# Batches of two, four and four chunks, all prepared ahead of v: a change of order in a hybrid DeltaNet and retention layer

## The chip, the cores and the metric

The kernel runs on one core of one Trainium2 chip. A core has a matrix engine (PE, with its weight loads shown apart as PEld), a vector engine (DVE), a scalar engine (ACT), a general engine (POOL) and a queue engine (SP) that mostly issues DMAs. The metric is the device time in microseconds of one execution; the time of a kernel is the median of its runs.

## The reference

One layer of a diffusion backbone: 256 context tokens and 1024 latent tokens of width 1024, all in fp32. What matters here is group A of the mixer, the gated delta rule with four heads of width 128, run in both directions:

```
qkv_a = short_conv(qkv_a, conv_w)          # 5 taps, then silu; context and latents apart
q, k, v = split(qkv_a)                     # (T, 4, 128) each
q = l2_normalize(q) * HEAD_DIM ** -0.5;  k = l2_normalize(k)
A   = strict_lower(kb @ k.T * decay)       # per chunk and head, kb = beta * k
u, w = solve(I + A, [v * beta, kb * exp(G)])
v_new = u - w @ S                          # a scan over the chunks
o     = q_dec @ S + (q @ k.T * decay) @ v_new
S     = g_last * S + k_dec.T @ v_new
```

Group B is a retention over the same tokens, with rotary angles on its q and k (`rq`, `rk`). Both groups get a norm and a gate (`z` for group A, `rg` for B), then follow an output projection, a residual, a SwiGLU feed-forward and a last norm.

## The kernel before

The kernel uses chunks of 128 tokens: chunks 0 and 1 are the context, 2 to 9 the latents. The forward scan takes 0, 1, 2 ... 9, the backward scan 1, 0, 9 ... 2. The inverse of I + A is computed for every chunk, head and direction, in batches of chunks, in four kinds of steps:

- `pre(t)`, line 719, prepares a chunk: it loads k (`kc`) and, for latents, q (`qc`), multiplies k with k (`kk`, line 724) and q with k (`kq`, line 729) on PE; for each direction it loads a broadcast row of decays (`gw`, 732), masks it on POOL (736), takes its exponential on ACT (740), multiplies on DVE (`ut`, 744, and `sp`, 746) and stores `ut` into the DRAM tensor `un` of its batch and `sp` into the packed scan input `sd`.
- `invert(b)`, line 757, loads the diagonal 32x32 blocks of the batch, one block per partition (`yr`, 765), copies them into `L` (772 on ACT, 773 on DVE) and solves them all at once on DVE: 31 steps of a multiplication (779) and a subtraction (781) whose row length depends on the step and not on the number of chunks. A copy `XT` (783) and four stores into `xd` end it.
- `merge(b)`, line 806, loads `un` into `U` (797) and the block inverses into `U` and `t64` (801, 802; each row piece of these two and of `yr` is 32 numbers long), and builds the whole inverse from the blocks by small matmuls (821 to 848) with evacuations on DVE and ACT. It ends with a store into `sd`.
- `solve(b)`, line 855, is `pre` for each chunk of the batch, then `invert`.

Between them stand the four convolution blocks of v (`conv_block(8 + h, ...)`, 866): projection matmuls from `hhi`, `hlo` with split weights (606 to 608), two copies on ACT (609, 610), four more taps on DVE (616), Silu on ACT (619), transpositions on PE (870), copies (872) and stores. Then come the token-major projections: the gate `z` (groups 8 and 9), the first two scan steps, `rk` (2 and 3) and `rq` (4 and 5). They share the PSUM tag `pa` (three banks) with v's transpositions; preparation and merges take tag `pb` (three), the convolution `pc` (two).

Order. The text gives each instruction its place; a planner at build time (`schedule_with_timeline_sim=True`, line 1665) orders every engine's instructions by a simulated timeline, so work from further down can be filled in where an engine would stand still. On the chip each engine then takes its instructions in that fixed order. Buffers come from pools that are opened and closed in the text; a new pool can lie where a closed one lay, and its tiles then wait for those that were there.

In the text before, the order is `solve(0)`, `solve(1)`, the four blocks of v, `pre` of batch 2, `merge(0)`, `invert(2)`, `merge(1)`, `merge(2)`, then `z`. The batches are [0, 1, 2, 9], [3, 8, 4, 7] and [5, 6]. The pool `GP` holds the preparation's buffers, `GI` those of the inverses. The merges' pool `GM` lies on the right side, where v's pool `CV` was; a further pool `G2` on the left holds `U` and `t64` of batch 1, so that two merges have buffers at once.

Of the kernel before, what the change touches and what calls it, by code (L numbers as in the profile page):

```python
# [8 lines left out]
F32 = mybir.dt.float32  # L9
# [8 lines left out]
P = 128  # L18
# [7 lines left out]
H = 4  # L26
# [12 lines left out]
def build(nc, tc, ap, dbg=None, stop=None, marks=None):  # L39
# [3 lines left out]
    def pool(name, bufs=1, side=None, space=None):  # L43
        kw = {}
        if side is not None:
            kw["side"] = side
        if space is not None:
            kw["space"] = space
        if space is not DRAM:
            kw["reuse_waits"] = "tile"  # L50
        es = ExitStack()
        p = es.enter_context(tc.tile_pool(name=name, bufs=bufs, **kw))
        root.push(es)
        p_close[id(p)] = es
        return p
# [3 lines left out]
    def close(p):  # L59
        p_close.pop(id(p)).close()  # L60
# [5 lines left out]
    def checkpoint(name):  # L66
        if dbg is not None:
            marks.append((name, int(nc.cur_bb.bb.instructions[-1].name.split("-")[-1])))
        if stop == name:
            raise Stop()  # L70
# [120 lines left out]
    try:  # L191
# [519 lines left out]
        GI = pool("gi")  # L711
        GP = pool("gp")

        BATCH = [[0,1,2,9],[3,8,4,7],[5,6]]
        where = {t: (b, c) for b, ch in enumerate(BATCH) for c, t in enumerate(ch)}

        un = [dr.tile([P, 2, len(ch) * H, P], F32, tag="un%d" % b, name="un%d" % b) for b, ch in enumerate(BATCH)]

        def pre(t):
            b, c = where[t]  # L720
            kc = load(GP, kd[t], "kc", 2)
            pk = bank_b("kk")
            for h in range(H):
                T.matmul(pk[:, h * P:(h + 1) * P], kc[:, h, :], kc[:, h, :], start=True, stop=True)
            if t >= 2:
                qc = load(GP, qd[t - 2], "qc", 2)
                pq = bank_b("kq")
                for h in range(H):
                    T.matmul(pq[:, h * P:(h + 1) * P], kc[:, h, :], qc[:, h, :], start=True, stop=True)
            for d in range(2):  # L730
                gw = GP.tile([P, H, P], F32, tag="gw", name="gw", bufs=2)
                SY.dma_start(gw.rearrange("p h i -> p (h i)"),
                             grow_d[c8(t, d), :].rearrange("a b -> (a b)").partition_broadcast(P))
                e = GP.tile([P, H, P], F32, tag="e", name="e", bufs=2)
                sg = 1 if d == 0 else -1
                G.affine_select(out=e, in_=gw, compare_op=ALU.is_ge, fill=FAR, base=0,
                                pattern=[[0, H], [sg, P]], channel_multiplier=-sg)
                for h in range(H):
                    col = t * 8 + d * 4 + h
                    S.activation(e[:, h, :], e[:, h, :], AF.Exp, bias=sm["nG"][:, col:col + 1])  # L740
                if t >= 2:
                    sp = GP.tile([P, 2, H, P], F32, tag="sp", name="sp", bufs=2)
                ut = GU.tile([P, H, P], F32, tag="ut", name="ut", bufs=2)
                V.tensor_tensor(ut.rearrange("p h i -> p (h i)"), pk, e.rearrange("p h i -> p (h i)"), ALU.mult)
                if t >= 2:
                    V.tensor_tensor(sp[:, 0].rearrange("p h i -> p (h i)"), pq, e.rearrange("p h i -> p (h i)"), ALU.mult)
                SY.dma_start(un[b][:, 1 - d, c * H:(c + 1) * H, :], ut)
                if t >= 2:
                    S.activation(gw, gw, AF.Exp)
                    G.tensor_tensor(sp[:, 1], gw, qc, ALU.mult)  # L750
                    SY.dma_start(sd[t, :, 8 - 8 * d:10 - 8 * d], sp.rearrange("p a h i -> p a (h i)"))
# [5 lines left out]
        def invert(b):  # L757

            nc_ = len(BATCH[b])
            nu = nc_ * H  # L760
            nb = 4 * nu
            xd = xds[b] = dr.tile([4 * nb, 1024], F32, tag="xd%d" % b, name="xd%d" % b)
            yr = GI.tile([P, 1024], F32, tag="yr", name="yr", bufs=1)
            for k in range(4):
                SY.dma_start(yr[k:2 * nb:4].rearrange("r (i j) -> r i j", j=32),
                             un[b][q32[k]].rearrange("i e u j -> (e u) i j")[:, :, q32[k]])
            L = GI.tile([P, 1024], F32, tag="L", name="L", bufs=3)
            X = GI.tile([P, 1024], F32, tag="X", name="X", bufs=2)
            G.memset(X, 0.0)
            G.memset(X[:, 0::33], 1.0)  # L770
            m = lambda t: t[:2 * nb].rearrange("p (i j) -> p i j", j=32)
            S.activation(L[:nb], yr[:nb], AF.Copy)
            V.tensor_copy(m(L)[nb:], yr[nb:2 * nb].rearrange("p (i j) -> p j i", j=32))
            for j in range(31):
                n = 31 - j
                tmp = GI.tile([P, 256], F32, tag="tmp%d" % b, name="tmp", bufs=2)
                t3 = tmp[:2 * nb, :n * (j + 1)].rearrange("p (i c) -> p i c", c=j + 1)
                sh = [2 * nb, n, j + 1]
                V.tensor_tensor(t3, bc(m(L)[:, j + 1:, j], sh, 2), bc(m(X)[:, j, :j + 1], sh, 1), ALU.mult)
                xs = m(X)[:, j + 1:, :j + 1]  # L780
                V.tensor_tensor(xs, xs, t3, ALU.subtract)
            XT = GI.tile([P, 1024], F32, tag="L", name="XT", bufs=3)
            V.tensor_copy(m(XT), X[:2 * nb].rearrange("p (i j) -> p j i", j=32))
            for i, x in enumerate((X[:nb], XT[nb:2 * nb], X[nb:2 * nb], XT[:nb])):
                SY.dma_start(xd[i * nb:(i + 1) * nb], x)

        def blocks(b):

            nu = len(BATCH[b]) * H
            nb = 4 * nu  # L790

            def blk(dram, k):
                return dram.rearrange("(u b) (i j) -> b i u j", b=4, j=32)[k]

            at = G2 if b == 1 else GM
            uu = at.tile([P, 2, len(BATCH[b]), H, P], F32, tag="U", name="U%d" % b, bufs=1)
            SY.dma_start(uu.rearrange("p e c h j -> p e (c h) j"), un[b])
            tt = at.tile([P, 2, nu, 64], F32, tag="t64", name="t64", bufs=1)
            G.memset(tt, 0.0)
            for k in range(4):  # L800
                SY.dma_start(uu[q32[k]].rearrange("p e c h j -> p (e c h) j")[:, :, q32[k]], blk(xds[b][:2 * nb], k))
                SY.dma_start(tt[q32[k]].rearrange("p e u j -> p (e u) j")[:, :, (k % 2) * 32:(k % 2) * 32 + 32],
                             blk(xds[b][2 * nb:], k))
            return uu, [uu[:, 1 - d] for d in range(2)], [tt[:, d] for d in range(2)]

        def merge(b):

            uu, ub, t64 = blocks(b)
            nu = len(BATCH[b]) * H
            q = q32  # L810
# [28 lines left out]
            for n0 in range(0, nu, 8):  # L839
                ps1, ps2 = bank_b("m2"), bank_b("m2")  # L840
                xt2 = GM.tile([P, 8, 64], F32, tag="xt2", name="xt2", bufs=1)
                for n in range(8):
# [12 lines left out]
        def solve(b):  # L855
            for t in BATCH[b]:
                pre(t)
            checkpoint("pre%d" % b)
            invert(b)
            checkpoint("inv%d" % b)  # L860

        solve(0)
        solve(1)
        for h in range(H):
            y = newy()
            conv_block(8 + h, y, False)
            for t0, n in ((0, 2), (2, 4), (6, 4)):
                ps = bank_a("vT")
                for t in range(t0, t0 + n):
                    T.transpose(ps[:, (t - t0) * P:(t - t0 + 1) * P], y[:, t * P:(t + 1) * P], ident)  # L870
                vt = CV.tile([P, 4, P], F32, tag="vt", name="vt", bufs=2)
                S.activation(vt[:, :n], ps[:, :n * P].rearrange("p (t j) -> p t j", j=P), AF.Copy)
                S.dma_start(vd[t0:t0 + n, :, h, :].rearrange("t p j -> p t j"), vt[:, :n])
# [1 line left out]
        checkpoint("v")  # L875
        RP = pool("rp", side="right")
        rope = RP.tile([P, TT, P], F32, tag="rope", name="rope")
        GM = pool("gm", side="right")
        for t in BATCH[2]:
            pre(t)  # L880
        close(GP)
        G2 = pool("g2")
        checkpoint("pre2")
        merge(0)
        SY.dma_start(rope, ap["rope"])
        invert(2)
        checkpoint("inv2")
        merge(1)
        merge(2)


        for g in (8, 9):
            token_major(g, LAT, fin_gate, S, W)
        checkpoint("rgz")
        close(GM)
        close(G2)
        close(GI)
        close(GU)

# [769 lines left out]
```

## Time and profile before

| what | us |
|---|---|
| median of 3 runs | 1480.59 |
| lowest and highest | 1477.06, 1481.09 |
| the profiled execution | 1480.75 |
| its span, first to last instruction | 1479.0 |
| mean granted PE clock | 0.98 |
| first chunk's `kk` on PE | 277.6 |
| v's last transposition on PE | 380.65 |
| first and last matmul of the merges (821, 848) | 409.5, 481.2 |
| end of the token-major projections | 580.6 |

A row of a timeline gives the start, the length, the engine, the line, the operation with the tile that it writes and those that it reads, and in brackets how long the engine stood idle before it and what released it. A row of a group gives the count, the busy time, the mean in ns, and the idle time ahead of the group.

### The profile page before, as it was taken

To read this page: it belongs to the slowest core of one execution; us is meant where nothing else is said; L and a number is where in the kernel's file an instruction comes from. 1 tells how busy PE (TensorE), PEld (TensorE's weight loads), DVE (VectorE), ACT (ScalarE), POOL (GpSimd) and SP (SyncE) were. 2 spreads that over 40 slices of the span, in tenths; PEclk is the share of its full clock that TensorE was granted. 3 is DMA by queue.
4 is the path that set the end of the run, shared out by engine and by line. 5 is a ranking of instruction groups with operands and counts; after the bars stand their busy time and mean duration, and the time that the engine had idled before them with its cause. 6 is when DMAs were issued, how large, how long until landed. Compare 5 with 4: busy or idle time off the path is not lost.

```text
span 1479.0 us, 24137 instructions
## 1 busy us (share of the span) xinstructions
PE 1401.6 (95%) x8919; PEld 1203.8 (81%) x8919; DVE 981.9 (66%) x1900; ACT 609.3 (41%) x1298; POOL 594.6 (40%) x501
## 2 busy tenths in 40 slices
PE   7999999988789999899799899999999999999997
PEld 2898888877779999899688688878888888788886
DVE  6568797379883445589777777646555564657486
ACT  5543554766322111236543533323333332454454
POOL 0120010244202354235144588899555553335331
PEclk9999999999799999999999899999999999999999
DMA  9536686698978823996633265765223242786863
GB/s 336 197 105 225 182 242 201 189 274 256 309 176 251 308 75 106 412 387 221 200 114 115 86 229 206 263 238 175 107 108 107 107 150 78 236 284 188 302 207 114
DMA packets 170422, 298.15 MB, mean 202 GB/s; under 512 B 43496, under 2 KB 93880, under 8 KB 165952
## 3 DMA queue, kind: packets, MB, share of 16 engines
q1 hardware_dynamic: 118752, 253.17, 50.3%
q10 hardware_dynamic: 49072, 35.83, 7.8%
q0 software_dynamic: 2480, 7.60, 1.4%
q8 instruction: 70, 1.15, 0.3%
q14 instruction: 48, 0.39, 0.1%
HBM read 206.60 MB, written 89.96 MB: 201 GB/s over the span
## 4 chain that ended last, share of the span: by engine, by line
PE 57%; DMA 6%; POOL 5%; DVE 4%; issue 2%; ACT 2%; SPq 0%; ACTq 0%; POOLq 0%; DVEq 0%
PE ffn L1358 7%; PE ffn L1356 7%; PE ffn L1357 7%; PE fo L1482 5%; PE fo L1484 5%; PE fo L1483 5%; PE tm L372 3%; PE tm L371 3%; PE tm L373 3%; PE op L1215 2%; PE op L1216 2%; PE op L1217 2%; PE Tr L935 1%; POOL ws L1329 1%; PE up L942 1%
## 5 line engine op out<-in xcount | busy, mean ns | idle before, releaser
L372 PE MATMUL tm<-wlo,hhi 128*128 128x256 f32 (+1 forms) x704 | 200.0, 287 | 4.6 <-issue 2.4
L371 PE MATMUL tm<-whi,hhi 128*128 128x256 f32 (+1 forms) x704 | 199.2, 288 | 4.7 <-ACT xa L384 1.9
L373 PE MATMUL tm<-whi,hlo 128*128 128x256 f32 (+1 forms) x704 | 197.9, 286 | 0.0
L344 ACT ACTIVATE whi<-wraw 128x512 fp32r<-128x512 f32 (+2 forms) x98 | 75.1, 771 | 162.9 <-PE ffn L1357 83.5
L371 PEld LDWEIGHTS tm<-whi,hhi 128*128 128x128 f32 x704 | 133.1, 191 | 8.6 <-ACT xa L384 2.5
L1356 PE MATMUL ffn<-t,whi 128*128 128x512 f32 x352 | 137.5, 392 | 1.2 <-ACT whi L344 1.2
L372 PEld LDWEIGHTS tm<-wlo,hhi 128*128 128x128 f32 x704 | 134.3, 191 | 4.3 <-DVE wlo L345 2.9
L1358 PE MATMUL ffn<-t,wlo 128*128 128x512 f32 x352 | 137.3, 391 | 0.4 <-DVE wlo L345 0.4
L1357 PE MATMUL ffn<-t,whi 128*128 128x512 f32 x352 | 137.7, 391 | 0.0
L373 PEld LDWEIGHTS tm<-whi,hlo 128*128 128x128 f32 x704 | 133.5, 191 | 3.1 <-issue 2.3
L344 ACT ACTIVATE whi<-ws 128x512 fp32r<-128x512 f32 x88 | 55.6, 632 | 171.5 <-PE ffn L1357 127.2
L345 DVE TENSOR_TENSOR wlo<-ws,whi 128x512 fp32r<-128x512 f32 x88 | 92.9, 1056 | 45.8 <-ACT whi L344 45.6
L1482 PE MATMUL fo<-whi,ahi 128*128 128x512 f32 x308 | 119.3, 390 | 0.7 <-ACT ahi L344 0.7
L1483 PE MATMUL fo<-wlo,ahi 128*128 128x512 f32 x308 | 119.9, 389 | 0.0
L1484 PE MATMUL fo<-whi,alo 128*128 128x512 f32 x308 | 119.0, 390 | 0.0
L345 DVE TENSOR_TENSOR wlo<-wraw,whi 128x512 fp32r<-128x512 f32 (+2 forms) x92 | 101.8, 1108 | 20.6 <-ACT whi L344 20.3
L1356 PE MATMUL ffn<-b,whi 128*128 128x512 f32 x264 | 104.3, 395 | 4.7 <-ACT whi L344 4.7
L1358 PE MATMUL ffn<-b,wlo 128*128 128x512 f32 x264 | 104.1, 394 | 1.2 <-DVE wlo L345 1.2
L1357 PE MATMUL ffn<-b,whi 128*128 128x512 f32 x264 | 103.9, 394 | 0.0
L606 PE MATMUL b<-hhi,whi 128*128 128x512 f32 (+1 forms) x256 | 94.3, 368 | 1.4 <-ACT y L610 1.4
L608 PE MATMUL b<-hhi,wlo 128*128 128x512 f32 (+1 forms) x256 | 94.7, 370 | 0.0
L607 PE MATMUL b<-hlo,whi 128*128 128x512 f32 (+1 forms) x256 | 93.9, 367 | 0.0
(450 smaller groups left out, 3460.1 us busy)
## 6 DMA issues: line engine op xcount, KB each, us to landing
adaw<-ada SPq DMA_DIRECT2D x48, 512.0 KB, 4.3
pk<-sd SPq DMA_DIRECT2D x16, 1536.0 KB, 12.5
wraw<-wfi SPq DMA_DIRECT2D x44, 512.0 KB, 3.5
ar<-ad SPq DMA_DIRECT2D x33, 512.0 KB, 4.8
w<-wfo SPq DMA_DIRECT2D x22, 512.0 KB, 5.8
wd<-tw SPq DMA_DIRECT2D x11, 1024.0 KB, 4.8
ad<-act SPq DMA_DIRECT2D x20, 512.0 KB, 3.0
raw<-wd SPq DMA_DIRECT2D x20, 512.0 KB, 5.0
```

The costliest lines, as they stand in the source:

```text
L344: S.activation(hi, raw, AF.Copy)
L345: e.tensor_tensor(lo, raw, hi.bitcast(F32), ALU.subtract)
L371: T.matmul(o, hhi[:, k, tsl], whi[:, k % 4, :], start=(k == 0), stop=False)
L372: T.matmul(o, hhi[:, k, tsl], wlo[:, k % 4, :], start=False, stop=False)
L373: T.matmul(o, hlo[:, k, tsl], whi[:, k % 4, :], start=False, stop=(k == KT - 1))
L608: T.matmul(o, wlo[:, k, :], hh, start=False, stop=(k == KT - 1))
L1356: T.matmul(o, whi[:, k, :], xhi(xn, slice(0, 4), k), start=(first and k == 0), stop=False, **kw)
L1357: T.matmul(o, whi[:, k, :], xlo(xn, slice(0, 4), k), start=False, stop=False, **kw)
L1358: T.matmul(o, wlo[:, k, :], xhi(xn, slice(0, 4), k), start=False, stop=(k == 3), **kw)
L1482: T.matmul(po[g][i], ahi[:, ts], whi, start=(j == 0 and not kw), stop=False, **kw)
L1483: T.matmul(po[g][i], ahi[:, ts], wlo, start=False, stop=False, **kw)
L1484: T.matmul(po[g][i], alo[:, ts], whi, start=False, stop=(j == FH - 1), **kw)
```

## The change

The batches become [0, 1], [2, 9, 3, 8] and [4, 7, 5, 6]. The preparation of batch 2, all merges and `invert(2)` move in the text from behind v to ahead of it. `GM` opens on the left, where `GP` was, and holds the buffers of all three merges; `G2` is gone, so there is one buffer for `U` and one for `t64`. The load of the rotary table stands alone between v and `z`.

```
-        BATCH = [[0,1,2,9],[3,8,4,7],[5,6]]
+        BATCH = [[0, 1], [2, 9, 3, 8], [4, 7, 5, 6]]
...
-            at = G2 if b == 1 else GM
-            uu = at.tile([P, 2, len(BATCH[b]), H, P], F32, tag="U", name="U%d" % b, bufs=1)
+            uu = GM.tile([P, 2, len(BATCH[b]), H, P], F32, tag="U", name="U%d" % b, bufs=1)
...
-            tt = at.tile([P, 2, nu, 64], F32, tag="t64", name="t64", bufs=1)
+            tt = GM.tile([P, 2, nu, 64], F32, tag="t64", name="t64", bufs=1)
...
         solve(0)
         solve(1)
+        for t in BATCH[2]:
+            pre(t)
+        close(GP)
+        GM = pool("gm")
+        checkpoint("pre2")
+        merge(0)
+        invert(2)
+        checkpoint("inv2")
+        merge(1)
+        merge(2)
         for h in range(H):
             y = newy()
             conv_block(8 + h, y, False)
...
         RP = pool("rp", side="right")
         rope = RP.tile([P, TT, P], F32, tag="rope", name="rope")
-        GM = pool("gm", side="right")
-        for t in BATCH[2]:
-            pre(t)
-        close(GP)
-        G2 = pool("g2")
-        checkpoint("pre2")
-        merge(0)
         SY.dma_start(rope, ap["rope"])
-        invert(2)
-        checkpoint("inv2")
-        merge(1)
-        merge(2)
...
         close(GM)
-        close(G2)
```

## The prediction, made before the changed kernel ran

> **What bounds the kernel now.** I read the busy times first, then windows over the stretch that the change touches, then who waited for whom there, then the timelines of the engines around the longest wait.
>
> ```profile
> PE 1401.6 (95%) x8919; PEld 1203.8 (81%) x8919; DVE 981.9 (66%) x1900; ACT 609.3 (41%) x1298; POOL 594.6 (40%) x501
> 280.00:380.00 100.00, 79.61 (x443) 69.36 (x441) 81.38 (x121) 66.46 (x146) 40.40 (x36) 0.89 0.88 272
> 382.00:482.00 100.00, 91.99 (x1667) 88.08 (x1667) 63.31 (x167) 27.91 (x52) 13.81 (x23) 0.95 0.83 238
> 482.00:582.00 100.00, 100.00 (x858) 100.00 (x857) 42.72 (x134) 10.52 (x14) 46.08 (x88) 1.00 0.40 147
> 290.00:310.00 20.00, 18.14 (x101) 16.09 (x100) 9.33 (x14) 10.73 (x27) 8.73 (x8) 0.91 0.86 260
> 310.00:330.00 20.00, 17.98 (x102) 15.19 (x100) 19.52 (x29) 15.12 (x30) 10.29 (x9) 1.00 0.91 260
> 330.00:350.00 20.00, 17.74 (x102) 15.98 (x103) 19.76 (x34) 14.21 (x29) 7.09 (x6) 0.91 0.84 290
> 350.00:370.00 20.00, 16.32 (x79) 13.82 (x77) 19.16 (x28) 12.49 (x25) 8.55 (x6) 0.87 0.86 239
> 370.00:390.00 20.00, 9.35 (x61) 9.35 (x62) 18.94 (x41) 9.59 (x18) 5.29 (x4) 0.61 0.99 338
> ```
>
> A windows row gives the stretch, its length, busy PE, weight loads, DVE, ACT and POOL, the granted clock, the DMA share and GB/s. The matrix engine PE is busy 95% of the span, so the time can only move by what its gaps do. Between 280 and 380 (prepare, first inverses, v) it is idle 20.4 us; between 382 and 482 (merges, gate z) 8.0; between 482 and 582 nothing. So from 382 to 582 a later start of that work is a later end, one for one. Ahead of it, DVE is full from 310 on (19.5, 19.8, 19.2, 18.9 of 20) and the DMA engines nearly so (0.84 to 0.99), but DVE has 10.7 us free in 290 to 310.
>
> ```profile
> PE vT L870 <- ACT y L619: 14.3, 2, 10.8
> 360.04 0.39 PE L608 MATMUL b<-hhi,wlo 128*128 128x512 f32 x1
> 365.71 2.40 PE L870 MATMUL vT<-ident,y 128*128 128x128 f32 x10 [3.50 <-ACT y L619]
> 367.90 1.92 PE L729 MATMUL kq<-qc,kc 128*128 128x128 f32 x8
> 380.65 2.40 PE L870 MATMUL vT<-ident,y 128*128 128x128 f32 x10 [10.84 <-ACT y L619]
> 382.70 0.56 PE L371 MATMUL tm<-whi,hhi 128*128 128x256 f32 x1
> 367.86 1.22 DVE L345 TENSOR_TENSOR wlo<-wraw,whi 128x1024 fp32r<-128x1024 f32 x1
> ```
>
> This is the one large gap: PE waits 14.3 us for Silu of v's third and fourth heads before it can transpose them. z's weights are split at 369.08 (the DVE row), yet z's first product starts at 382.70, just behind the last transposition. Both take their PSUM bank from the tag `pa`, which has three, and one head's transpositions take all three; I infer from the code that z cannot pass v's last head. So **v's last transposition is the gate** of everything to 582, and the question is when it comes. I call its start (380.65) v's end.
>
> **The change part by part.** The time is worked from the profiled execution, 1480.75 us with a span of 1479.0; the median of the runs is 1480.59, 0.16 less.
>
> *What is not removed.* Ten chunks are still prepared, three inverses still run, ten chunks merged. An inverse step costs by its row length, not by its chunks:
>
> ```profile
> L779 DVE TENSOR_TENSOR tmp<-L,X 128x31 f32<-128x31 f32 (+23 forms) x93 | 37.4, 402 | 2.8
> L781 DVE TENSOR_TENSOR X<-X,tmp 128x31 f32<-128x31 f32 (+23 forms) x93 | 35.5, 382 | 2.6
> 316.78 1.12 DVE L773 COPY L<-yr 64x1024 f32<-64x1024 f32 x1
> 383.88 1.10 DVE L783 COPY XT<-X 128x1024 f32<-128x1024 f32 x1
> 385.01 1.10 DVE L773 COPY L<-yr 64x1024 f32<-64x1024 f32 x1
> 416.50 1.11 DVE L783 COPY XT<-X 128x1024 f32<-128x1024 f32 x1
> 376.83 0.68 DVE L744 TENSOR_TENSOR ut<-kk,e 128x512 f32<-128x512 f32 x1
> 378.03 1.27 DVE L616 SCALAR_TENSOR_TENSOR y<-u,cw,y 128x1022 f32<-128x1022 f32 x1
> ```
>
> Three times 62 steps, 72.9 us, before and after: 0. The first inverse ran from 316.78 to 385 among v's taps, the second nearly alone from 385.01 to 417.6, 32.6 us.
>
> *Inverses ahead of v's taps.* The order of each engine comes from a planner that reads the text's order as priority and fills in other work where it sees room: v's last tap (378.03) ran ahead of the second inverse (385.01), which the text puts first. A batch of two chunks without q is complete after the second chunk, so I take the first inverse to begin about 17 us sooner, near 300. Half of DVE is free there: some 5 us are swallowed. The rest runs beside the first head's taps and lets the second inverse, which before begins behind v's end, put steps ahead of the last taps. The DVE is full from then on, so what is put ahead of v's last tap delays it by its own length. Bounds: nothing (the planner keeps the taps where they are) and a whole inverse less the free room, 32.6 - 10.7 = 21.9 us. I take +5: some 20 steps at 0.39 us (72.9 over 186) and two copies at 1.1 come to 10 us, less the 5 swallowed. It lies near the lower end, since in the rows before, taps and steps shared the engine about one to one.
>
> *Chunks 5 and 6 ahead of v.* Before, they stood behind v in the text; now all ten stand ahead of it. A chunk takes two passes, each a broadcast load of gw, a mask on POOL, exponentials on ACT, products on PE and DVE:
>
> ```profile
>   DMA gw<-grow_d: 28.7, 10
> 361.28 1.28 ACT L740 ACTIVATE e<-e,nG 128x128 f32<-128x128 f32 x4 [3.70 <-POOL e L736]
> 366.51 0.58 ACT L609 ACTIVATE u<-b 128x512 f32<-128x512 f32 x1
> 366.99 0.68 ACT L610 ACTIVATE y<-b,cw 128x512 f32<-128x512 f32 x1
> 375.13 1.28 ACT L619 ACT_TABLE_LOAD   x1
> 379.33 1.27 ACT L619 ACTIVATE y<-y 128x1280 f32<-128x1280 f32 x1 [2.92 <-DVE y L616]
> 349.01 0.50 PE L606 MATMUL b<-hhi,whi 128*128 128x512 f32 x1 [1.37 <-ACT y L610]
> ```
>
> Waits for gw sum to 28.7 us, in ten places. v's last matmul ended at 360.43 but its copy began at 366.51: ACT took its instructions in their order, and the preparation's exponentials (idle 3.70 us for POOL's mask) stood ahead. v's own chain from there to the transposition is 1.26 (two copies) + 4 x 1.27 (taps) + 2.55 (table and Silu) = 8.9 us; it took 20.2. Early bound: if all preparation is past by then, v's end is 360.43 + 8.9 + three steps between the taps, 1.1, = 370.4, a gain of 10.2. Late bound: the last head's two long chunks (349.01 to 360.43, 11.4 us) and its chain come behind the last preparation (377.5): 397.8, a loss of 17.2. Which, depends on where the planner sees gw land. I take +3: the new priority puts four more passes ahead of v in queues that serve in order, against a DMA share of 0.84 to 0.99 that lets no pass come much sooner. Behind a late pass wait ACT's copies of v, hence both PSUM banks of the convolution, hence PE.
>
> *Merges, and where they lie.*
>
> ```profile
> 395.27 10.67 SPq L802 DMA_DIRECT2D t<-xd  x4
> 405.99 3.20 SPq L801 DMA_DIRECT2D U<-xd  x4
> 481.13 2.05 PE L935 MATMUL Tr<-pk 128*128 128x128 f32 x16
> L372 PE MATMUL tm<-wlo,hhi x704: 274/282/415, 38.8 to 580.5; 128*128 128x256 f32 x156, 128*128 128x272 f32 x20
> 585.95 11.62 DMA pk<-sd
> ```
>
> The merges lose their second U buffer: each must store before the next loads. Their load's issues took 13.9 us of SP (10.67 + 3.20), so two exposed loads make 28 us more in that chain, at most. The chain releases the first scan step (481.13), but token-major products fill PE until 580.5, and the scan is waited for only from 585.95: 100 us of cover. Price 0; without the cover up to 28. SP is passed by the merges' loads ahead of rope and of the scan's pk loads; both have the same cover. POOL clears t64 for the second merge behind the first; the head weights that POOL splits for v and rope's sums queue there, but are due earlier or under that cover: 0. Merges beside v could put matmuls into the gap: the first needs the preparation's buffers, free from 377.5, and a load, so hardly before v's end: 0, at best its own few us of small matmuls.
>
> *The gap's clock.*
>
> ```profile
> 383.49 0.41 PE L371 MATMUL tm<-whi,hhi 128*128 128x256 f32 x1
> 383.70 0.41 PE L372 MATMUL tm<-wlo,hhi 128*128 128x256 f32 x1
> 385.77 0.28 PE L371 MATMUL tm<-whi,hhi 128*128 128x256 f32 x1
> 385.88 0.28 PE L372 MATMUL tm<-wlo,hhi 128*128 128x256 f32 x1
> ```
>
> After the gap matmuls start 0.21 us apart, by 385.77 they are at 0.11: of the 3.07 us between, at most half, some 1.4 us, is lost, once. A longer gap loses no more, and it is in the time already: 0. The Trainium skill ("TensorE: Matmul & The Clock Gate", Part 1: The HAM clock gate) says that an idle window of about 3.4 us drops PE to half clock until about 3.4 us of work have passed. By that rule a gap that the change splits in two long pieces would cost an estimated 1.7 us more, and the sum would be 1490.5; the trace agrees in kind, with under 3.07 us of slow work behind a gap of 10.84.
>
> *Sum.* +5 +3 and the rest 0: v's end near 388.7, and 1480.75 + 8 = 1488.75, **1489 us**.
>
> **The rivals.** *A, the tail comes free (faster).* The planner gets the preparation out of the way before v's last head is due, and its 8.9 us chain runs almost alone: the early bound, -10.2, gives 1470.5. For it: the tail of 20.2 us is more than half foreign work. Against it: the DMA share, and a DVE that is already full. It decides if the last e of the preparation leaves ACT before v's last matmul ends. *B, nothing moves (same).* The planner fills as before; the gate stays v's last head and its order against the preparation comes out alike, as preparation already runs at one pace: the gap only gets other names. 1481. *C, much slower, within my forecast's side:* the last head falls wholly behind the preparation, +17.2, and inverse steps add the 5: 1503.
>
> **How the numbers follow.** About 0.3% (4.4 us) is what a measurement of this kernel can tell from no change. Forecast, later v by 5 to 17: 0.40. C: 0.06. B: 0.23. A: 0.31. So slower 0.46, same 0.23, faster 0.31. As both signs are likely, the range runs from A's 1470.5, less 4 for merges that fill what is left of the gap, to C's 1503: 1466 to 1503. The forecast's own range is 1485 to 1498.
>
> **What would show it.** In the changed profile: the last vT row and its wait for Silu (right: start near 389, a wait of 10 us or more; A: near 370, a wait under 5); z's first product right behind it; the first L copy near 300 and the second before the last tap; the last ut against v's last copy on ACT; PE full from z's first product to the last rope product; the first Tr of the scan well before 580. It is wrong if z starts ahead of v's last head (then the bank is no gate), if merges or inverses open new PE gaps behind v's end larger than 8 us, or if the end of the token-major products moves otherwise than v's end does.

## The result and the profile after

| | us |
|---|---|
| before, median of 4 runs beside it | 1478.82 (1477.04 to 1481.09) |
| after, median of 4 runs | 1495.05 (1491.42 to 1496.17) |
| ratio | 1.0105, 95% interval [1.008, 1.013] |
| profiled execution after | 1491.42, span 1489.4 |

The changed kernel is slower by 1.05%. The median lies 6.3 us above the forecast of 1488.75; the profiled execution, which is the lowest of the four, lies 2.7 above it. What the other three spend more, 3.6 to 4.8 us, no trace shows.

First the busy times of after:

```profile
PE 1401.9 (94%) x8919; PEld 1202.6 (81%) x8919; DVE 976.9 (66%) x1900; ACT 608.8 (41%) x1298; POOL 597.2 (40%) x501
```

PE has the same work: 1401.9 us busy, 1401.6 before. So a longer span can only be more idle time, and the next step is to find where it lies. The windows of before and then of after, from v's stage to the end of the read-out (stretch, its length, busy PE, weight loads, DVE, ACT, POOL, granted clock, DMA share, GB/s):

```profile
300.00:400.00 100.00, 79.52 (x470) 71.72 (x469) 92.04 (x158) 59.51 (x119) 38.77 (x32) 0.86 0.90 278
400.00:600.00 200.00, 189.51 (x2510) 184.73 (x2510) 102.17 (x309) 40.72 (x69) 62.50 (x113) 0.98 0.62 196
600.00:720.00 120.00, 108.69 (x907) 103.82 (x906) 101.25 (x365) 54.83 (x164) 39.22 (x36) 0.99 0.86 319
720.00:1100.00 380.00, 368.36 (x1645) 302.40 (x1644) 252.36 (x351) 136.90 (x241) 262.24 (x177) 0.98 0.48 168
```

```profile
300.00:400.00 100.00, 70.82 (x419) 61.93 (x418) 90.93 (x154) 59.48 (x120) 42.61 (x32) 0.86 0.83 255
400.00:600.00 200.00, 190.67 (x2514) 186.43 (x2514) 95.16 (x275) 39.23 (x66) 57.48 (x110) 0.97 0.62 199
600.00:720.00 120.00, 108.85 (x923) 106.20 (x922) 100.78 (x368) 50.38 (x154) 41.05 (x38) 0.98 0.86 320
720.00:1100.00 380.00, 365.75 (x1637) 299.21 (x1636) 249.60 (x370) 139.54 (x249) 260.36 (x176) 0.98 0.49 172
```

Length less busy PE is PE's idle time: 20.5 before and 29.2 after in 300 to 400, so 8.7 of the 10.4 us that the span grew are lost there; 2.6 more are lost in 720 to 1100; behind v, from 400 to 600, it even fell from 10.5 to 9.3. The waits of PE in after's 300 to 400 (total, times, longest) and rows of its timelines:

```profile
PE vT L879 <- ACT y L619: 17.3, 3, 13.1
PE kq L729 <- DVE ut L744: 9.0, 2, 6.7
```

```profile
308.62 1.62 PE L729 MATMUL kq<-qc,kc 128*128 128x128 f32 x6 [6.65 <-DVE ut L744]
387.44 2.39 PE L879 MATMUL vT<-ident,y 128*128 128x128 f32 x10 [13.11 <-ACT y L619]
389.48 0.56 PE L371 MATMUL tm<-whi,hhi 128*128 128x256 f32 x1
296.71 1.12 DVE L773 COPY L<-yr 32x1024 f32<-32x1024 f32 x1 [3.58 <-DMA yr<-un]
374.12 1.04 DVE L773 COPY L<-yr 64x1024 f32<-64x1024 f32 x1
```

v's last transposition starts at 387.44, 6.8 us later than before (380.65), and z's first product still stands right behind it. Three more rows of after tell where the 6.8 us arise:

```profile
365.86 0.40 PE L608 MATMUL b<-hhi,wlo 128*128 128x512 f32 x1
383.00 1.28 ACT L740 ACTIVATE e<-e,nG 128x128 f32<-128x128 f32 x4 [4.78 <-POOL e L736]
386.11 1.27 ACT L619 ACTIVATE y<-y 128x1280 f32<-128x1280 f32 x1
```

v's last matmul ends at 366.26, 5.8 us later than before (360.43), so most of the shift is there before v's tail begins. The tail itself, from that matmul to v's end, takes 21.2 us where before took 20.2. In it Silu starts at 386.11 although v's last tap ended at 384.23: ACT first ran the last exponentials of the preparation, for which it had waited 4.78 us, and a table load behind them. A gap of 6.65 us has opened much earlier, at 302, where PE waits for `ut` of chunk 9 to free its bank. Chunk 9 is the fourth chunk of the preparation and the second with q; the expectations below call its two `ut` the third pair.

### The profile page after: what moved, and what is told of

Read it like the earlier page. It is cut to its first block, busy times and chain, and to the rows that moved or that the text cites. A ratio compares the mean times of both kernels' runs of the same rounds, so it can differ in the third digit from the quotient of the medians.

```text
span 1489.4 us, 24135 instructions
## 1 busy us (share of the span) xinstructions
PE 1401.9 (94%) x8919; PEld 1202.6 (81%) x8919; DVE 976.9 (66%) x1900; ACT 608.8 (41%) x1298; POOL 597.2 (40%) x501
## 4 chain that ended last, share of the span: by engine, by line
PE 44%; DMA 11%; DVE 8%; POOL 5%; issue 5%; ACT 3%; SPq 0%; ACTq 0%; POOLq 0%; DVEq 0%
PE ffn L1353 7%; PE ffn L1351 7%; PE ffn L1352 7%; DMA ar<-ad 3%; PE tm L372 3%; PE tm L373 3%; PE tm L371 3%; DVE wlo L345 2%; PE op L1210 2%; PE op L1212 2%; PE op L1211 2%; DMA wd<-tw 1%; DMA raw<-wd 1%; DMA pk<-sd 1%; DMA raw<-wfo 1%
```

## What made chunk 9 late

SP's queue around that gap, before and then after (start, length of the issue, line, transfer, count):

```profile
290.83 0.32 SPq L747 DMA_DIRECT2D un<-ut  x1
291.46 0.32 SPq L751 DMA_DIRECT2D sd<-sp  x1
291.87 0.40 SPq L732 DMA_DIRECT2D gw<-grow_d  x1
292.36 0.77 SPq L747 DMA_DIRECT2D un<-ut  x1
293.24 0.40 SPq L751 DMA_DIRECT2D sd<-sp  x1
293.72 0.44 SPq L732 DMA_DIRECT2D gw<-grow_d  x1
```

```profile
291.35 2.62 SPq L765 DMA_DIRECT2D yr<-un  x4
294.06 0.56 SPq L747 DMA_DIRECT2D un<-ut  x1
294.72 1.20 SPq L751 DMA_DIRECT2D sd<-sp  x1
295.97 0.42 SPq L747 DMA_DIRECT2D un<-ut  x1
296.50 0.73 SPq L751 DMA_DIRECT2D sd<-sp  x1
297.32 1.85 SPq L732 DMA_DIRECT2D gw<-grow_d  x2
```

Before, each `gw` load of chunk 9 went out between chunk 2's stores, the first at 291.87. After, the first inverse is due once its two chunks are done, its loads of `yr` take 2.62 us of issue, and both `gw` loads stand behind all four stores of chunk 2, at 297.32. The mask and the first `ut` of chunk 9, before and then after:

```profile
296.65 0.64 POOL L736 TENSOR_SCALAR_AFFINE_SELECT e<-gw 128x512 f32<-128x512 f32 x1 [3.63 <-DMA gw<-grow_d]
298.69 0.69 DVE L744 TENSOR_TENSOR ut<-kk,e 128x512 f32<-128x512 f32 x1 [6.10 <-ACT e L740]
```

```profile
303.81 1.22 POOL L736 TENSOR_SCALAR_AFFINE_SELECT e<-gw 128x512 f32<-128x512 f32 x2 [10.19 <-DVE X L781]
305.84 0.69 DVE L744 TENSOR_TENSOR ut<-kk,e 128x512 f32<-128x512 f32 x1 [2.14 <-ACT e L740]
```

Both moved by 7.2 us, about as far as v's end. (The releaser "DVE X" of POOL's row is a name that e10 below does away with.) Whether this shift is what moves v's end, or the inverse steps on DVE that the prediction counted on, or something behind v, is what the first experiments ask.

## Experiments on the preparation

**e9: more buffers for gw.**

```diff
-                gw = GP.tile([P, H, P], F32, tag="gw", name="gw", bufs=2)
+                gw = GP.tile([P, H, P], F32, tag="gw", name="gw", bufs=4)
```

> The changed kernel with four buffers for gw in place of two, which lets SP issue chunk 9's two loads of gw ahead of chunk 2's stores. Theory Q (preparation's order on SP sets v's end): the PE gap of 6.65 us ahead of the third pair of ut goes under 3, the third pair of ut is at 299 to 303, v's last transposition near 381, and the time falls by about 6 to 1489. Theory D (inverse steps on a full DVE ahead of v's taps set v's end): the gap may go, but v's end stays at 385 or later and the time at 1492 or more.

Measured: 1487.94 (1484.34 to 1488.64), ratio to before 1.0052 [1.0036, 1.0069], where the changed kernel had 1.0105 [1.008, 1.013]. Its timelines:

```profile
296.82 0.69 DVE L744 TENSOR_TENSOR ut<-kk,e 128x512 f32<-128x512 f32 x1
305.83 1.13 PE L724 MATMUL kk<-kc 128*128 128x128 f32 x8 [2.91 <-DMA kc<-sd]
380.20 2.40 PE L879 MATMUL vT<-ident,y 128*128 128x128 f32 x10 [8.98 <-ACT y L619]
```

The 6.65 us gap is gone (2.91 is left, for another load), chunk 9's first `ut` comes at 296.8, v's end is back at 380.2, before's place, and PE's idle time in 300 to 400 falls from 29.2 to 21.8. Half of the loss in time is gone; the other half, 7.7 us over before, remains although v's end is back. (The profiled execution gained only 3.5 us on that of after, the median 7.1: of the 7.4 us of idle time, 2.6 came back in 400 to 600 and 1.4 as busy time.) The edit frees every chunk's `gw`, not chunk 9's alone: v's last matmul ends 2.8 us sooner than in after (363.44), and the tail shrinks to 16.8 us, since the preparation's last exponentials leave ACT at 366.2, ahead of v's last copies. So what it shows is that the preparation's pace through these two buffers sets v's end, and not that chunk 9 alone does.

**e10: the first inverse without its steps.**

```diff
-            for j in range(31):
+            for j in range(31 if b else 0):
```

> The changed kernel without the 31 steps of the first inverse (62 DVE instructions, about 24 us); its loads, copies and stores stay. Theory D: those steps stand in DVE's way to v's taps, so v's last transposition comes 5 us sooner or more, at 382 or earlier, and the time falls by as much, though the PE gap near 302 stays. Theory Q: v's end stays within 2 us of 387.4, as the gap near 302 stays and v's taps find room on DVE anyway; the time stays within 3 of 1495.

Measured: 1499.48 (1498.16 to 1504.13), ratio 1.0137 [1.0112, 1.0162]. The window 300 to 360 of e10, then two rows of its timelines; after had 52.69 us of DVE in that window:

```profile
300.00:360.00 60.00, 51.10 (x272) 43.76 (x271) 42.11 (x55) 40.88 (x85) 24.03 (x21) 0.91 0.83 269
```

```profile
304.84 0.69 DVE L744 TENSOR_TENSOR ut<-kk,e 128x512 f32<-128x512 f32 x1 [6.08 <-POOL e L736]
385.99 2.40 PE L879 MATMUL vT<-ident,y 128*128 128x128 f32 x10 [15.46 <-ACT y L619]
```

With 62 DVE instructions left out and 10.6 us less DVE work in the window, chunk 9 is as late as in after and v's end moves by 1.4 us. So the first inverse's steps did not hold v's taps back. The second inverse moved up (its first `L` copy at 347.1 in place of 374.1), but it doesn't fill their place: 27 inverse steps, 12.0 us, run ahead of v's last tap in e10, where before has 47 (26.8 us), after 65 (28.6) and e9 61 (34.3). v's end does not follow these numbers: e9 has nearly as many as after and ends v 7.2 us sooner. DVE's idle 6.08 us ahead of `ut` shows that the mask is what is late. That e10 is slower than after though it does less comes from further on: its profiled execution has 6.8 us more idle time of PE in 720 to 1100, where the read-out waits 7.4 us for DVE, and 5.2 us more of busy time.

**e1: the first yr loads issued by ACT.**

```diff
-                SY.dma_start(yr[k:2 * nb:4].rearrange("r (i j) -> r i j", j=32),
+                (S if b == 0 else SY).dma_start(yr[k:2 * nb:4].rearrange("r (i j) -> r i j", j=32),
```

> The changed kernel, but the four loads of the first inverse (yr of batch 0) are issued by ACT instead of SP; nothing else. Theory Q (queue): in the changed kernel these loads stand on SP ahead of the stores and the gw loads of chunk 2, wait there until 291.35 for the stores of ut, and hold the whole preparation back by about 7 us, which v's end inherits. Then the third pair of ut products comes near 299 to 301 instead of 305.8, v's last transposition near 380 instead of 387.4, and the time falls by 5 to 8 us from the changed kernel's 1495 to 1487 to 1490. Rival D (my prediction's step: DVE steps ahead of the taps): the inverse steps stay where they are, so v's end stays within 2 us of 387 and the time within 3 us of 1495. A third outcome, that ACT now waits for ut's stores in SP's place, would leave the delay and move it to ACT's e.

Measured: 1503.77 (1501.28 to 1509.55), ratio 1.0167 [1.0137, 1.0196]. The queue, POOL and DVE of e1 in order of engine:

```profile
292.74 2.30 SPq L732 DMA_DIRECT2D gw<-grow_d  x2
298.89 1.79 POOL L736 TENSOR_SCALAR_AFFINE_SELECT e<-gw 128x512 f32<-128x512 f32 x2 [6.76 <-DMA gw<-grow_d]
302.07 1.26 POOL L750 TENSOR_TENSOR sp<-gw,qc 128x512 f32<-128x512 f32 x1 [1.38 <-ACT gw L749]
303.75 1.28 POOL L750 TENSOR_TENSOR sp<-gw,qc 128x512 f32<-128x512 f32 x1 [0.42 <-POOL sp L750]
301.83 0.27 DVE L779 TENSOR_TENSOR tmp<-L,X 64x112 f32<-64x112 f32 x1
302.13 1.33 DVE L781 TENSOR_TENSOR X<-X,tmp 64x112 f32<-64x112 f32 x1
303.82 1.36 DVE L781 TENSOR_TENSOR X<-X,tmp 64x135 f32<-64x135 f32 x1
305.10 0.67 DVE L744 TENSOR_TENSOR ut<-kk,e 128x512 f32<-128x512 f32 x1
```

SP is 4.6 us earlier with `gw`, as it should be. But the inverse steps stand ahead of chunk 9's `ut` in DVE's fixed order and start only when `yr` has landed (first `L` copy at 298.49), so `ut` comes at 305.10 all the same. One wait had taken another's place; v's end is 389.5. Here, unlike in after, it is inverse steps that hold `ut`.

**e5: gw issued by ACT.**

```diff
-                SY.dma_start(gw.rearrange("p h i -> p (h i)"),
+                S.dma_start(gw.rearrange("p h i -> p (h i)"),
```

> The changed kernel with one edit: the broadcast loads of gw are issued by ACT and no longer by SP. Theory Q (SP's order in the preparation): in the changed kernel both loads of gw for the third pair of ut stand on SP behind the stores un, sd, un, sd of the pair before, and PE waits 6.65 us there, which moves v's end by 6.8. Then here the third pair of ut comes near 299 to 303 in place of 305.8, no PE gap ahead of it is over 3 us, v's last transposition starts near 381, and the time falls by about 6 to 1489. Theory M (the loss is made behind v's end, by merges from a single U buffer): preparation may move but the time stays at 1495 +-3. A third outcome: gw lands early but qc and kc, still on SP behind the same stores, take its place as what is late; then the gap stays and is named kc, qc or sp.

Measured: 1495.95 (1494.38 to 1498.36), ratio 1.0105 [1.0083, 1.0126]: no gain. ACT issued the loads at 294.31, behind its own exponentials. Chunk 9's first `ut` came at 301.63 and the gap shrank to 3.61 us, but PE then waited 4.2 us for another `kq`, and v's end stayed at 387.6: the third outcome, in kind. An earlier chunk 9 alone did not bring v's end back.

**e8: the first inverse behind four chunks.**

```diff
-        solve(0)
-        solve(1)
+        for t in (0, 1, 2, 9):
+            pre(t)
+        invert(0)
+        for t in (3, 8):
+            pre(t)
+        invert(1)
```

> The changed kernel with its new batches, but chunks 0, 1, 2, 9 prepared ahead of the first inverse, then 3 and 8, then the second inverse. Theory Q: the early loads of yr and the stores around them are what disorders SP, so with the first inverse behind four chunks the third pair of ut is at 299 to 303, v's end near 381, and the time about 1488. Theory M: 1495 +-3 with v's end earlier all the same. Third: the preparation meets another late load and v's end stays at 387 or later.

Measured: 1495.84 (1494.49 to 1496.52), ratio 1.0098 [1.008, 1.0115]. Chunk 9's `ut` come at 300.0 and 302.9 and the gap there is 2.41, as expected; v's end came only to 384.6, and the time did not move, for a reason that lies far behind v (next section).

**e4: v's transpositions in another PSUM tag.**

```diff
-                ps = bank_a("vT")
+                ps = bank_c("vT")
```

> The changed kernel with v's transpositions in the convolution's PSUM tag (two banks) instead of the one that z's products take (three). If v's last transposition is the gate of z because of the shared banks, z's first products now run ahead of it, PE's wait of 13.1 us for v's Silu shrinks below 5, and the time falls by 5 to 10 us to 1485 to 1490, for all theories of why v ends late. If the gate is no matter of the banks (z's weights, or the planner's order), z still starts behind the last transposition and the time stays within 3 us of 1495. As the convolution and its transpositions now share two banks, v may itself become slower by a few us.

Measured: 1506.49 (1502.15 to 1507.8), ratio 1.0174 [1.015, 1.0199]. PE's first product of z and v's last transposition in e4:

```profile
382.71 0.62 PE L371 MATMUL tm<-whi,hhi 128*128 128x256 f32 x3 [0.91 <-ACT whi L344]
438.45 0.44 PE L879 MATMUL vT<-ident,y 128*128 128x128 f32 x2
```

With the bank changed, z's products pass v's last head by 55 us. So the bank was indeed what kept z behind v. It did not pay: the preparation got gaps of 9.6, 9.7 and 10.8 us in its place.

## Experiments on the order behind v

These kernels differ in text order or batches. For all of them the idle time of PE is worked out as above, span less busy PE and stretch by stretch, from the windows of each:

| kernel | v's end | busy | idle | 300:400 | 400:600 | 600:720 | 720:1100 |
|---|---|---|---|---|---|---|---|
| before | 380.7 | 1401.6 | 77.4 | 20.5 | 10.5 | 11.3 | 11.6 |
| after | 387.4 | 1401.9 | 87.5 | 29.2 | 9.3 | 11.2 | 14.2 |
| e2, order alone | 381.7 | 1402.1 | 85.6 | 22.9 | 10.0 | 12.2 | 16.7 |
| e3, batches alone | 374.8 | 1407.2 | 83.5 | 19.2 | 16.9 | 10.2 | 14.6 |
| e6, merges behind v | 385.3 | 1400.4 | 84.0 | 28.1 | 9.2 | 10.6 | 13.7 |
| e7, z first | 378.8 | 1402.7 | 80.7 | 20.9 | 4.7 | 17.2 | 13.4 |
| e8, inverse late | 384.6 | 1402.5 | 90.8 | 23.3 | 11.6 | 10.5 | 20.6 |
| e9, four gw | 380.2 | 1403.3 | 82.5 | 21.8 | 11.9 | 10.5 | 14.2 |
| e12, fewer chunks ahead | 379.2 | 1400.8 | 89.1 | 23.2 | 16.4 | 11.2 | 13.8 |

**e2: the changed order with the old batches.**

```diff
-        BATCH = [[0, 1], [2, 9, 3, 8], [4, 7, 5, 6]]
+        BATCH = [[0, 1, 2, 9], [3, 8, 4, 7], [5, 6]]
```

> The changed text order (all preparation and all merges ahead of v, one U buffer on the left) with the batches of before, four, four and two. Theory Q: SP's order up to chunk 9 is that of before, so no 7 us at 291; v's end near 381 to 383; what is left is the text order's own price behind v's end (merges with one buffer), 0 to 4 us: 1479 to 1485. Rival P (my prediction's step: chunks 5 and 6 ahead of v, in queues that serve in order, cost v's tail): v's end 384 or later and 1484 to 1490. Rival D gives 1481: the first inverse starts where it did.

Measured: 1490.79 (1487.16 to 1497.55), ratio 1.0077 [1.0051, 1.0102]. All ten chunks stand ahead of v, and v's end is 1.0 us later than before: with the old batches, moving chunks 5 and 6 and the merges ahead of v costs v's end no more than that. The loss lies elsewhere. PE's row in the read-out, and two of SP's rows, the scan's last stores and the load that PE waits for (the loads of `yt` and `xl` stand between them):

```profile
725.57 0.77 PE L1092 MATMUL ro<-vg,pm 128*128 128x128 f32 x2 [7.50 <-DMA vg<-rd]
```

```profile
706.43 7.12 SPq L975 DMA_DIRECT2D dy<-yo  x2
721.16 0.33 SPq L660 DMA_DIRECT2D vg<-rd  x1
```

The last load of the read-out stands on SP behind the scan's last stores. e1 (10.5 us) and e8 (10.2) have the same wait; before, after and e6 have not.

**e11: e2 with the read-out's vg loads on ACT.**

```diff
-            vg = load(RT, rd[t, :, 2:4], "vg", 4, (P, 2, 512))
+            vg = RT.tile([P, 2, 512], F32, tag="vg", name="vg", bufs=4)
+            S.dma_start(vg, rd[t, :, 2:4])
```

> e2_old_batches (the changed order with the old batches, 1490.79) with one edit: the loads of vg for the latent chunks of the read-out are issued by ACT. In e2 the last of them stood on SP behind the scan's last store, and PE waited 7.50 us for it; v's end was only 1 us later than in before. If that wait is where e2's loss lies, the time falls by about 7 to 1483, and e2's rest over before is 2 to 4 us. Rival: another wait takes its place, on ACT or in the read-out, and the time stays at 1488 or more.

Measured: 1492.62 (1487.84 to 1494.32), ratio 1.008 [1.0054, 1.0106]. The same row in e11:

```profile
728.47 0.76 PE L1093 MATMUL ro<-vg,pm 128*128 128x128 f32 x2 [5.98 <-DVE rru L137]
```

The rival held. The load was only the wait that came last; behind it stands a chain on DVE that ends nearly as late. e2's later loss is the end of the read-out, not one queue. Why that end comes out worse in this order stays open.

**e6: merges and third inverse back behind v.**

```diff
-        GM = pool("gm")
         checkpoint("pre2")
-        merge(0)
-        invert(2)
-        checkpoint("inv2")
-        merge(1)
-        merge(2)
...
         rope = RP.tile([P, TT, P], F32, tag="rope", name="rope")
+        GM = pool("gm", side="right")
+        merge(0)
         SY.dma_start(rope, ap["rope"])
+        invert(2)
+        checkpoint("inv2")
+        merge(1)
+        merge(2)
```

> The changed kernel with the merges and the third inverse put back behind v in the text; the new batches stay, all ten chunks are prepared ahead of v, and there is one U buffer, now opened behind v. Theory Q: preparation and the first two inverses are as in the changed kernel, so v's end stays near 387 and the time near 1495 (1490 to 1498). Theory M (merges ahead of v in the text bring scan work and stalls forward): PE gaps behind v's end fall under 5 us in all and the time to about 1485 or less. If a single U buffer is what costs, gaps named for U stay at 2 us or more with their place changed.

Measured: 1489.72 (1486.17 to 1491.5), ratio 1.0054 [1.0033, 1.0076]. Neither expectation was met as written: v's end comes 2.2 us sooner (385.3), and the time falls by some 5 us. The table shows no single place: 1.1 less in 300 to 400, 0.6 and 0.5 less further on, and 1.5 less of busy time. So the place of the merges and of the third inverse in the text, with the merges' buffers on the other side, costs about half a per cent; which wait it sits in is not shown.

**e3: the new batches in the old order.** 

```diff
-        BATCH = [[0,1,2,9],[3,8,4,7],[5,6]]
+        BATCH = [[0, 1], [2, 9, 3, 8], [4, 7, 5, 6]]
```

> The text order and buffers of before with the new batches two, four and four, so that chunks 4, 7, 5, 6 stand behind v and the first inverse starts early. Theory Q: the same four loads stand ahead of chunk 2's gw on SP, so the third pair of ut comes near 305 as in the changed kernel; v, having only six chunks ahead of it, may still end no later than 388: 1483 to 1492. Rival P: with four chunks instead of two behind v, v's tail is freer than before and the time is 1470 to 1479. Rival D: 1484 to 1490.

Measured: 1497.25 (1492.85 to 1501.38), ratio 1.0126 [1.0093, 1.0159]. v's end is 5.9 us earlier than in before and the kernel is slower. PE's waits in 400 to 600, the first two by size ("issue" means that the profile names no releaser):

```profile
PE m L828 <- issue: 5.0, 1, 5.0
PE Tr L935 <- DMA pk<-sd: 3.9, 1, 3.9
```

Four chunks are now merged behind the last inverse, and my reading is that both the merges and the scan's first products stand on PE, in its fixed order, before they can run; for the merges' wait the profile doesn't say so. Idle time there rises by 6.4 us, and the granted clock in that window falls from 0.98 to 0.93, which goes with 5.6 us more of busy time. Chunk 9's first `ut` comes at 303.8 here, nearly as late as in after, and v still ends early: with four chunks fewer ahead of v, a late chunk 9 does not make v late.

**e12: before, with the second batch behind v.**

```diff
         solve(0)
-        solve(1)
...
+        solve(1)
         for t in BATCH[2]:
             pre(t)
```

> The kernel before with the second batch (3, 8, 4, 7) prepared and inverted behind v in the text, so that four chunks stand ahead of v and not eight. Theory N (v's end goes by the number of chunks ahead of it; with the new batches six gave 374.8 and ten 387.4, 3.15 us a chunk): v's end near 368. If the preparation behind it hides beside z, the time falls by some 10, to 1470. Rival: as with the new batches in the old order, the merges come later and PE gets gaps behind v's end and at the scan's first steps; then v's end is early and the time is 1482 or more.

Measured: 1494.38 (1491.63 to 1496.13), ratio 1.0095 [1.0073, 1.0117]. Theory N fell: with four chunks ahead of v in the text in place of eight, v's end is 379.2, only 1.5 us earlier. The planner spreads what it has; the count of chunks does not set v's end. The rest went as the rival said: 5.9 us more idle time in 400 to 600, where the merges' loads of `t64` alone are waited for 6.5 us.

**e7: before, with z ahead of the merges.**

```diff
+        SY.dma_start(rope, ap["rope"])
+        for g in (8, 9):
+            token_major(g, LAT, fin_gate, S, W)
         merge(0)
-        SY.dma_start(rope, ap["rope"])
         invert(2)
```

> The kernel before, with z's two groups put ahead of the merges in the text. In before, PE has 8.0 us of gaps behind v's end, the largest 3.9 and 2.4, while z's products lie open for it. If the text's order decides who has the first call on PE there, z's products run first and merges fill; the gaps fall to under 3 us and the time by about 5, to 1474, as the scan has some 100 us of cover. Rival: the planner fills the same gaps already and the merges' evacuations come later; then the first Tr moves behind 500 and the time is 1479 or more.

Measured: 1482.37 (1473.08 to 1488.57, 10 runs), ratio 1.001 [0.9988, 1.0032]. The two windows behind v of e7:

```profile
400.00:600.00 200.00, 195.34 (x2544) 189.71 (x2543) 105.55 (x323) 41.27 (x69) 61.44 (x113) 0.97 0.62 201
600.00:720.00 120.00, 102.85 (x850) 99.53 (x848) 96.03 (x329) 50.30 (x155) 37.34 (x34) 0.96 0.78 292
```

The gaps behind v close as expected (10.5 to 4.7), and all of it is given back one stage later (11.3 to 17.2), where scan and read-out wait for DVE. None of these kernels beats before.

## Why the prediction was right, and where it was not

- **The gate.** "v's last transposition is the gate of everything to 582": right for z's start. z's first product stands 2.0 us behind it in after, and e4 shows the bank as the reason. That a shift of v's end is a shift of the end "one for one" does not hold: in e3 and e12 v ends 5.9 and 1.5 us sooner than in before, and both are slower. And the prediction named it as a sign of being wrong if the end of the token-major products moves otherwise than v's end. It did: the last one starts at 594.3 in place of 580.6, 13.7 us later against 6.8. More scan work lies ahead of that end, 48 products `kS` where before had 32, so this end is no measure of time lost.
- **v's end near 388.7**: measured 387.4.
- **"Inverses ahead of v's taps", +5: the step that failed.** The first `L` copy came at 296.7 and the second at 374.1, as foretold, but e10, with 38 inverse steps fewer ahead of v's last tap, has v's end at 386.0, only 1.4 us sooner. Between v's last copy on ACT and its last tap, inverse work took DVE 3.5 us in after and 3.0 in before, so in the tail the term came to under half a us. I had put DVE's fullness ahead of the queue.
- **"Chunks 5 and 6 ahead of v", +3**: not measured alone. e2 gives 1.0 for the whole new order with the old batches. In after, the exponentials of the last chunk, with the table load behind them, held Silu back by 1.9 us (384.23 to 386.11), a wait on ACT of the kind that the prediction named.
- **What stood in their place**: an early first inverse puts `yr` loads into SP's queue and lets SP's order push chunk 9's `gw` behind chunk 2's stores. The shift of 6.8 us at v's end goes away with four `gw` buffers (e9), and 5.8 of it stood already at v's last matmul, ahead of the tail. That chunk 9's delay alone passes on to v's end is not shown: e5 and e8 bring its first `ut` 4.2 and 5.9 us sooner, and v's end comes 0.1 later and 2.9 sooner. Shown is that the preparation waits for its `gw` buffers and that v's end waits for the preparation. The prediction named in-order queues, but for the wrong chunks; that its two terms add to 8 and the shift is 6.8 is luck in the parts.
- **Merges, 0**: little idle time was added behind v: 9.3 against 10.5 in 400 to 600, and 9.5 against 8.0 from z's first product to the last token-major one. The reload into the single `U` cost one wait of 2.2 us. But e6 shows that their place in the text, with that of the third inverse, costs some 5 us of time, so the 0 was too low.
- **The gap's clock, 0**: the granted clock in 300 to 400 is 0.86 in both. The rival price for a split gap, 1.7 us more, is too near to be told apart by these runs.
- **Rivals.** A, a free tail, did not come: the wait for Silu grew from 10.84 to 13.11. B, nothing moves, did not come, as v's end moved. C, wholly behind the preparation, did not either: the last `ut` (384.4) still ran behind v's last tap.
- **The size.** 8 us were forecast. The profiled execution grew by 10.7, the median by 16.2. In the traces 8.7 us are idle time of PE in 300 to 400, most of it v's shift of 6.8, and 2.6 lie in the stretch from 720 to 1100. The median's other 5.6 us have no trace: the median of after lies 3.6 above its profiled execution, that of before 1.9 below. By medians, e9 gives back 7.1 and e6 5.3; the two edits were not tried together, so whether these add up is open. The range and the direction held; about half of the size was missed.

## What to carry to other kernels

Where a planner orders each engine's queue, moving a step moves its DMA issues too: look at the issuing queue's order around the moved step, above all for a load with few buffers that now stands behind stores which wait. Add idle time of the bottleneck stage by stage before believing that a gap closed is time won: e3 and e7 closed gaps of 1 to 6 us, and gave them back one stage later. Two more buffers for a small, late load did more here (e9) than issuing it from another queue (e5).

## What the runs showed of the hardware

In e1's rows the DVE step of 64x112 at 302.13 took 1.33 us, and the one before it on the same shape 0.27. It ends just behind POOL's product that ran from 302.07 to 303.33; the next stretched step, 303.82 to 305.18, lies over POOL's 303.75 to 305.03. So two-operand steps on DVE stood still while POOL multiplied. In before, POOL's memset of `t64` (392.26 to 394.07), which reads nothing, ran beside steps of 0.39 to 0.41 us, as long as such steps take without it. The Trainium skill ("SBUF — State Buffer", SBUF: two separate sides) says that a DVE instruction with two SBUF inputs and a GpSimd one that reads SBUF exclude each other for a whole instruction; these rows agree. Reading work moved onto an idle POOL is thus not free for DVE.
